# A trunk of convolution, attention and gated layers: layer norm read from PSUM, two output jobs side by side, one PSUM layout

## The chip, the core and the metric

The kernel runs on one core of a Trainium2 chip. A core has a matrix engine (PE, whose weight loads stand apart as PEld), a vector engine (DVE), a scalar engine (ACT), a general engine (POOL) and a queue engine that starts transfers (SP). Each works through its own queue of instructions in order and waits for the others by semaphores. SBUF is the working memory; PSUM is the small memory that the matrix engine writes its sums to, eight banks of 512 numbers of 4 bytes in each of 128 partitions. POOL cannot read or write PSUM in this kernel's program: all its operands lie in SBUF.

The metric is the time of one execution on the device, in microseconds (us). Lower is better.

## What is computed

The input is 256 positions of 2048 features. There is one convolution layer with its gated feed-forward block, then keys and values, then one attention layer with its feed-forward block, and a last norm. The change lies in the convolution layer alone:

```python
def _conformer_conv(h, w1, b1, dw, dw_b, ln_g, ln_b, w2, b2):
    u = h @ w1 + b1
    a, gate = jnp.split(u, 2, axis=-1)
    u = a * jax.nn.sigmoid(gate)
    u = lax.conv_general_dilated(...) + dw_b
    u = jax.nn.silu(_layernorm(u, ln_g, ln_b))
    return u @ w2 + b2

def _layernorm(x, g, b):
    mu = jnp.mean(xf, axis=-1, keepdims=True)
    var = jnp.mean(jnp.square(xf - mu), axis=-1, keepdims=True)
    y = (xf - mu) * lax.rsqrt(var + LN_EPS) * g + b
```

The convolution runs over the positions, feature by feature, with 31 taps. Its layer norm needs every feature of a position, so that no number of z = silu(layernorm(...)) exists before the last tile of features has been through product, gate and convolution.

## The kernel before

Features lie on the partitions, in 16 tiles of 128; the 256 positions are the columns. All matrix products are of 4-byte numbers split in a high part (`hi`, cast by ACT on L168) and a rest (`lo`, made on L170 by DVE or POOL): three passes, hi by hi, hi by rest and rest by hi. The weights come in blocks of 512 KB, 4 tiles of inputs by 256 outputs, started by SP through a ring of four `raw` buffers, with three `whi` and three `wlo` buffers behind it. `next_block` hands out a block and prepares those up to two further on (`AHEAD`), in the order of the list `blocks`.

**First product (w1).** 16 jobs, j = 0 to 15, each of four blocks (L480, `project`, matmuls on L223). The first block of a job is native: its four tiles take one pass of unsplit weights (`rawn`). Job j makes 128 features and their 128 gates in one PSUM bank, `pp` of shape 128 x 2 x 256, and three such banks go round. Then `glu(bk, j)`, called with high priority: DVE scales the bank by the norm (L380), ACT makes the gate (L382), DVE multiplies and writes `up[:, j]` (L383). While the next job runs on PE, `conv(j)` works on `up[:, j]`: ACT starts two sums in PSUM (L409, `acc`, two tiles called `aux`), DVE adds 23 taps to them in turn (L411), ACT and POOL make six taps by products and a tree of sums (L423, L425, L442, L444), and DVE puts them together into `cT[:, j]` (L447). The last job differs: 16 taps go through PE with diagonal weights (L404) and 12 through ACT and DVE. `set_shift` (L455) sums `cT[:, 0]` on PE to get a shift that later tiles subtract, and `stats(j)` sums `cT[:, j]` and its squares over the features on PE (L474, L476, L478) into the tile `st`.

**Layer norm and z.** Behind the last statistics an order written out by hand holds for ACT, DVE and POOL: ACT copies the mean from PSUM to `mu` in SBUF (L509), DVE squares it and subtracts (L511, L512), ACT takes the root (L513), DVE and POOL subtract `mu` (L517; POOL takes the tiles 2 to 15 in seven pairs), DVE takes the reciprocal (L518). Then group after group (two single tiles, seven pairs): DVE scales (L522), ACT takes Silu (L530), ACT or DVE casts the high part of z (L531), DVE makes the rest (L532).

**Second product (w2).** Eight jobs u of four blocks (L341, matmuls on L227 and L229), each making 256 features in two banks, two such tiles going round; `residual` reads them (L331, L333). The stages behind it (feed-forward, attention, feed-forward) use the same `project`.

PSUM has two layouts, one after the other: three `pp` of one bank with five `aux`, then, from L534 on, two `pp` of two banks with four `aux`.

What the program as built waits for is a matter of the framework: it follows which instruction touches which part of a tile and puts a semaphore wait where two engines touch the same one. It also chooses the order of each engine's queue outside the part that is ordered by hand.

Of the kernel before, what the change touches and what calls it, by code (L numbers as in the profile page):

```python
# [12 lines left out]
ALU = mybir.AluOpType  # L13
# [66 lines left out]
def trunk(ctx: ExitStack, tc: tile.TileContext, xT, vec, const, w1, w2, wk, wv, wq, wo, wg0, wu0, wd0, wg1, wu1, wd1, out):  # L80
# [46 lines left out]
    for u in range(DT // 2):  # L127
        plan(w2, u, DT)
# [17 lines left out]
    def emit_block():  # L146
        i = len(ready)
        w, u, g, gk = blocks[i]
        shape = [P, gk, GK * NB // gk]
        native = NATIVE if w is w1 and g == 0 else 0  # L150
        if native:
            raw = conv_pool[0].tile(shape, F32, name="rawn", bufs=2)
        else:
            raw = wp.tile(shape, F32, name="raw", bufs=RAW)
        hi = lo = None
        if native < gk:
            hi = wp.tile(shape, F32R, name="whi", bufs=AHEAD + 1)
            lo = wp.tile(shape, F32R, name="wlo", bufs=AHEAD + 1)
        src = w[u, g].rearrange("p (k n) -> p k n", k=gk)
        step = gk if i >= DT // GK else 1 if i == 0 else 2  # L160
        for s in range(0, gk, step):
            if i < DT // GK:
                load_x(GK * g + s, step)
            part = slice(s, s + step)
            nc.sync.dma_start(raw[:, part, :], src[:, part, :])
            part = slice(max(s, native), s + step)
            if part.start < part.stop:
                nc.scalar.copy(hi[:, part, :], raw[:, part, :])  # L168
                eng = nc.gpsimd if (w is w1 and i >= 6) or (w is w2 and u == 0) else nc.vector
                eng.tensor_tensor(out=lo[:, part, :], in0=raw[:, part, :], in1=hi[:, part, :].bitcast(F32), op=ALU.subtract)  # L170
        ready.append((raw, hi, lo))
        if i == DT // GK - 1:
            x_loaded()

    def next_block(w, u, g):
        i = used[0]
        used[0] += 1
        assert blocks[i][:3] == (w, u, g)
        while len(ready) < min(len(blocks), i + 1 + AHEAD):
            emit_block()  # L180
        return ready[i]
# [18 lines left out]
    psum = []  # L200

    def bank2():
        return psum[-1].tile([P, 2, 2, S], F32, name="pp", bufs=2)

    def aux(shape):
        return psum[-1].tile(shape, F32, name="aux", bufs=4 if len(psum) > 1 else 5)

    def project(w, u, kt_n, x, xf=None):


        bk = psum[-1].tile([P, 2, S], F32, name="pp", bufs=3) if xf is not None else bank2()
# [20 lines left out]
        return bk  # L232

# [102 lines left out]
    def out_proj(w, kt_n, x, bias, g):  # L336

        nx = new_x(rp, "x")
        norm = Norm()
        for u in range(DT // 2):  # L340
            residual(project(w, u, kt_n, x), u, bias, norm)  # L341
            for i in (2 * u, 2 * u + 1):
                split_scaled(nx, i, v(g, i))
        return nx, norm
# [6 lines left out]
    with tc.tile_pool(name="cv", bufs=1) as cv, tc.tile_pool(name="cvu", bufs=1) as cvu:  # L351
        conv_psum = ExitStack()
        psum.append(conv_psum.enter_context(tc.tile_pool(name="psc", bufs=1, space=PSUM)))
# [37 lines left out]
        def conv(j):  # L391
# [3 lines left out]
            acc = [aux([P, S]) for _ in range(3 if n_pe else 2)]  # L395
# [17 lines left out]
            def products(lo, hi):  # L413
                for k in range(lo, hi):
# [5 lines left out]
                    else:  # L420
                        win, w = tap(TAPS - n_pool + k)
                        if k == 0:
                            nc.scalar.activation(dst, win, AF.Identity, scale=w, bias=v("dw_b", j))  # L423
                        else:
                            nc.scalar.activation(dst, win, AF.Copy, scale=w)  # L425

            def step(n):
# [3 lines left out]
                if n == 0 and n_pe:  # L431
                    on_pe()
                if n < 2:
                    products(*((0, 4) if n == 0 else (4, leaves)))
                for i in range(n_vec):
                    if i * 4 // n_vec == n:
# [21 lines left out]

        st = aux([P, 2, S])
# [20 lines left out]
        for j in range(DT):  # L480
            bk = project(w1, j, DT, x, xf)
# [13 lines left out]
            if j == DT - 1:  # L495
                table(AF.Sqrt, sigmoid)
# [4 lines left out]
        flush()  # L501

# [4 lines left out]
        with tc.manual_schedule(engines={mybir.EngineType.Activation, mybir.EngineType.DVE, mybir.EngineType.Pool}):  # L507
            mu = cv.tile([P, S], F32, name="mu")
            nc.scalar.copy(mu, st[:, 0, :])  # L509
            rl = sp.tile([P, S], F32, name="rstd")  # L510
            nc.vector.tensor_tensor(out=rl, in0=mu, in1=mu, op=ALU.mult)  # L511
            nc.vector.tensor_tensor(out=rl, in0=st[:, 1, :], in1=rl, op=ALU.subtract)  # L512
            nc.scalar.activation(rl, rl, AF.Sqrt, bias=ln_eps)  # L513
            groups = [(0, 1), (1, 1)] + [(j, 2) for j in range(2, DT, 2)]
            for j, n in groups:
                c2 = cT[:, j:j + n, :]
                (nc.vector if j < 2 else nc.gpsimd).tensor_tensor(out=c2, in0=c2, in1=_bc(mu, n), op=ALU.subtract)  # L517
            nc.vector.reciprocal(rl, rl)  # L518

            def scaled(j, n):  # L520
                c2 = cT[:, j:j + n, :]
                nc.vector.tensor_tensor(out=c2, in0=c2, in1=_bc(rl, n), op=ALU.mult)  # L522

            scaled(*groups[0])
            for i, (j, n) in enumerate(groups):
# [6 lines left out]
                nc.vector.tensor_tensor(out=z[:, j:j + n, 1, :], in0=c2, in1=z[:, j:j + n, 0, :].bitcast(F32), op=ALU.subtract)  # L532

        conv_psum.close()  # L534
        psum.append(ctx.enter_context(tc.tile_pool(name="ps", bufs=1, space=PSUM)))
        x, norm = out_proj(w2, DT, z, "b2", "f0_g")
# [178 lines left out]
```

## Time and profile before

| | us |
|---|---|
| median of 3 runs | 2209.11 (2209.0 to 2209.14) |
| the profiled execution | 2208.4 |
| its span in the trace | 2206.6 |
| PE busy | 2173.5 (98%) |
| DVE busy | 1297.3 (59%) |
| ACT busy | 1071.0 (49%) |
| POOL busy | 463.4 (21%) |

In a row of the timeline the first number is the start and the second the length in us; several equal instructions that follow each other are one row, with their count behind an x, and the square brackets tell how long the engine had been idle and who released it. The chain of waits goes back from the last instruction of the program, at each step to what it had waited for. An fp32 matmul of unsplit numbers stands twice in the records (x16 for 8).

### The profile page before, as it was taken

Reading aid. Unit: us, or ns where it says so; the run is one execution under the profiler, and the core shown is the slowest. Engines: PE = TensorE matmul, PEld = TensorE weight load, DVE = VectorE, ACT = ScalarE, POOL = GpSimd, SP = SyncE. Lnnn points to the kernel's source line nnn. Section 1 sums busy time; section 2 is a strip of 40 time slices with the busy share of each in tenths; the row PEclk is TensorE's granted clock in tenths of the full one; section 3 lists DMA queues with packets and bytes.
Section 4 is the critical chain, followed back from the end, with each engine's and each line's share of the span. In section 5 each row is a group of like instructions: output and inputs, shape, how many; then the busy total and the mean of one; then the engine's idle time right before and its main releaser. Section 6 shows DMA issues by size and latency. Waiting matters only on the chain.

```text
span 2206.6 us, 31780 instructions
## 1 busy us (share of the span) xinstructions
PE 2173.5 (98%) x12570; PEld 1916.9 (87%) x12570; DVE 1297.3 (59%) x1626; ACT 1071.0 (49%) x1393; POOL 463.4 (21%) x296
## 2 busy tenths in 40 slices
PE   8999799999999999999999999999999999999997
PEld 7999688888888888888888888888888888888886
DVE  7888876555555554555545677665555555544444
ACT  6666455444444444444444566454444444443442
POOL 5999211212121210000000100112121212100000
PEclk9999899999999999999999999999999999999999
DMA  6544355555555555555565544555555555555553
GB/s 235 172 167 158 106 187 185 190 185 189 190 188 189 187 191 190 186 188 190 181 192 192 188 143 136 189 190 186 188 190 189 186 188 190 189 187 188 191 190 125
DMA packets 112181, 401.41 MB, mean 182 GB/s; under 512 B 12576, under 2 KB 13728, under 8 KB 112032
## 3 DMA queue, kind: packets, MB, share of 16 engines
q1 hardware_dynamic: 111456, 398.57, 54.7%
q8 instruction: 98, 1.61, 0.3%
q10 hardware_dynamic: 576, 0.81, 0.1%
q14 instruction: 51, 0.42, 0.1%
HBM read 397.24 MB, written 2.10 MB: 181 GB/s over the span
## 4 chain that ended last, share of the span: by engine, by line
PE 97%; DVE 1%; issue 0%; ACT 0%; DMA 0%; SPq 0%; DVEq 0%; ACTq 0%
PE pp L227 54%; PE pp L229 28%; PE pp L223 8%; PE pp L262 1%; PE pp L264 1%; PE pp L263 1%; PE pp L245 1%; PE pp L247 0%; PE aux L598 0%; PE aux L593 0%; PE aux L575 0%; PE aux L474 0%; DVE x L278 0%; DMA hT<-xT 0%; DVE x L663 0%
## 5 line engine op out<-in xcount | busy, mean ns | idle before, releaser
L170 DVE TENSOR_TENSOR wlo<-raw,whi 128x1024 fp32r<-128x1024 f32 (+1 forms) x691 | 860.8, 1246 | 797.3 <-ACT whi L168 796.8
L168 ACT CAST whi<-raw 128x1024 fp32r<-128x1024 f32 (+1 forms) x739 | 772.7, 1046 | 1034.9 <-PE pp L227 816.7
L227 PE MATMUL pp<-x,whi 128*128 128x512 f32 x3328 | 839.4, 393 | 0.0
L227 PEld LDWEIGHTS pp<-x,whi 128*128 128x128 f32 x3328 | 599.4, 189 | 106.6
L229 PEld LDWEIGHTS pp<-x,wlo 128*128 128x128 f32 x3328 | 454.0, 190 | 32.4
L229 PE MATMUL pp<-x,wlo 128*128 128x256 f32 x3328 | 464.1, 282 | 0.0
L227 PE MATMUL pp<-hid,whi 128*128 128x512 f32 x1320 | 330.5, 392 | 0.0
L227 PEld LDWEIGHTS pp<-hid,whi 128*128 128x128 f32 x1320 | 237.4, 189 | 42.4
L300 POOL TENSOR_TENSOR sqacc<-sqacc,sq 128x512 f32<-128x512 f32 x30 | 50.6, 1688 | 711.5 <-ACT sq L296 701.6
L229 PEld LDWEIGHTS pp<-hid,wlo 128*128 128x128 f32 x1320 | 180.1, 190 | 12.9
L229 PE MATMUL pp<-hid,wlo 128*128 128x256 f32 x1320 | 184.1, 282 | 0.0
L553 POOL TENSOR_TENSOR hid<-t,hid 128x512 fp32r<-128x512 f32 x44 | 79.7, 1810 | 396.1 <-ACT hid L552 396.1
L411 DVE SCALAR_TENSOR_TENSOR aux<-up,vecs,aux 128x256 f32<-128x256 f32 x355 | 144.5, 480 | 3.4 <-ACT aux L409 3.4
L223 PE MATMUL pp<-x,whi 128*128 128x256 f32 x768 | 142.1, 287 | 1.1 <-ACT whi L168 1.1
L547 POOL TENSOR_TENSOR t<-t,rstd 128x512 f32<-128x512 f32 x44 | 57.0, 1297 | 352.8 <-DVE t L272 343.9
L223 PEld LDWEIGHTS pp<-x,whi 128*128 128x128 f32 x768 | 120.7, 191 | 2.4 <-ACT whi L168 1.5
L170 POOL TENSOR_TENSOR wlo<-raw,whi 128x1024 fp32r<-128x1024 f32 x48 | 114.0, 2390 | 24.4 <-DVE up L383 14.9
L223 PE MATMUL pp<-x,wlo 128*128 128x256 f32 x384 | 109.2, 284 | 4.9 <-DVE wlo L170 4.9
L223 PEld LDWEIGHTS pp<-x,wlo 128*128 128x128 f32 x384 | 73.5, 191 | 6.3 <-DVE wlo L170 5.9
L227 PE MATMUL pp<-z,whi 128*128 128x512 f32 x256 | 67.7, 406 | 10.8 <-DVE z L532 10.7
L272 DVE TENSOR_TENSOR t<-pp,t 128x512 f32<-128x512 f32 x104 | 71.0, 683 | 6.1 <-ACT t L271 6.1
L549 POOL TENSOR_TENSOR t<-t,rstd 128x512 f32<-128x512 f32 x44 | 65.3, 1484 | 34.3 <-ACT t L548 34.3
(130 smaller groups left out, 1505.7 us busy)
## 6 DMA issues: line engine op xcount, KB each, us to landing
raw<-wg SPq DMA_DIRECT2D x176, 512.0 KB, 3.3
raw<-wu SPq DMA_DIRECT2D x176, 512.0 KB, 3.3
raw<-wd SPq DMA_DIRECT2D x176, 512.0 KB, 3.3
raw<-w SPq DMA_DIRECT2D x77, 512.0 KB, 3.3
raw<-wv SPq DMA_DIRECT2D x32, 512.0 KB, 4.1
raw<-wk SPq DMA_DIRECT2D x32, 512.0 KB, 3.4
raw<-wq SPq DMA_DIRECT2D x32, 512.0 KB, 3.3
raw<-wo SPq DMA_DIRECT2D x32, 512.0 KB, 3.3
```

Source lines behind the costliest of these rows:

```text
L168: nc.scalar.copy(hi[:, part, :], raw[:, part, :])
L170: eng.tensor_tensor(out=lo[:, part, :], in0=raw[:, part, :], in1=hi[:, part, :].bitcast(F32), op=ALU.subtract)
L223: nc.tensor.matmul(bk[:, m, :], a[:, j, ws], b, start=first and m == 0 and i == 0, stop=last and i == len(passes) - 1, skip_group_check=True)
L227: nc.tensor.matmul(bk[:, m, :, :], hi[:, j, ws], x[:, kt, :, :], start=kt == 0, stop=False, skip_group_check=True)
L229: nc.tensor.matmul(bk[:, m, 0, :], lo[:, j, ws], x[:, kt, 0, :], start=False, stop=kt == kt_n - 1, skip_group_check=True)
L245: nc.tensor.matmul(bk[:, 0, :, :], hi[:, j, :], x[:, kt, :, :], start=kt == 0, stop=False, skip_group_check=True)
L272: nc.vector.tensor_tensor(out=t, in0=bk[:, :, 0, :], in1=t, op=ALU.add)
L300: add.tensor_tensor(out=self.acc, in0=self.acc, in1=sq, op=ALU.add)
L411: nc.vector.scalar_tensor_tensor(out=acc[i % 2], in0=win, scalar=w, in1=acc[i % 2], op0=ALU.mult, op1=ALU.add)
L547: nc.gpsimd.tensor_tensor(out=t, in0=t, in1=_bc(norm.r, 2), op=ALU.mult)
L549: nc.gpsimd.tensor_tensor(out=t, in0=t, in1=_bc(norm.r, 2), op=ALU.mult)
L553: nc.gpsimd.tensor_tensor(out=hid[:, 2 * u:2 * u + 2, 1, :], in0=o, in1=hid[:, 2 * u:2 * u + 2, 0, :].bitcast(F32), op=ALU.subtract)
```

## The change

- `psum` is one pool for the whole program: two `pp` of two banks and four `aux`. The convolution stage takes both `pp`: `jobs`, whose two halves (a bank each) serve the jobs j of w1 in turn, and `chains`, whose two banks hold the two tap sums of the odd j. The even j keep two `aux`.
- The first two jobs of w2 run side by side: their blocks alternate in the list, and `project_pair` is a generator that issues two tiles of inputs for both jobs at a time and is stepped once for each group of z behind the first. The blocks from the fourth of these eight on are prepared at five places in the loop over the groups; one more than before is prepared ahead of the statistics. Their `lo` parts are all made by POOL.
- The layer norm reads the mean (`st[:, 0, :]`) and the reciprocal deviation (`st[:, 1, :]`, where DVE now writes it) from PSUM in DVE's own steps. ACT squares the mean from PSUM; `mu` in SBUF stays for POOL's seven pairs.
- In the last convolution ACT starts the sums ahead of the products, and the load of the root's table moves from behind the last gate to behind the last product.
- `out_proj` takes the two finished jobs as `first`.

Nothing of the arithmetic is left out, and the number of matmuls and of transfers stays.

```diff
...
         plan(w1, u, DT)
-    for u in range(DT // 2):
+    for g in range(DT // GK):
+        blocks.extend((w2, u, g, GK) for u in range(2))
+    for u in range(2, DT // 2):
...
                 nc.scalar.copy(hi[:, part, :], raw[:, part, :])
-                eng = nc.gpsimd if (w is w1 and i >= 6) or (w is w2 and u == 0) else nc.vector
+                eng = nc.gpsimd if (w is w1 and i >= 6) or (w is w2 and u < 2) else nc.vector
...
-    def next_block(w, u, g):
+    def next_block(w, u, g, ahead=AHEAD):
...
         assert blocks[i][:3] == (w, u, g)
-        while len(ready) < min(len(blocks), i + 1 + AHEAD):
+        while len(ready) < min(len(blocks), i + 1 + ahead):
...
-    psum = []
+    psum = ctx.enter_context(tc.tile_pool(name="ps", bufs=1, space=PSUM))
     def bank2():
-        return psum[-1].tile([P, 2, 2, S], F32, name="pp", bufs=2)
+        return psum.tile([P, 2, 2, S], F32, name="pp", bufs=2)
     def aux(shape):
-        return psum[-1].tile(shape, F32, name="aux", bufs=4 if len(psum) > 1 else 5)
...
-    def project(w, u, kt_n, x, xf=None):
...
-        bk = psum[-1].tile([P, 2, S], F32, name="pp", bufs=3) if xf is not None else bank2()
+        return psum.tile(shape, F32, name="aux", bufs=4)
...
+    def project(w, u, kt_n, x, xf=None, bk=None):
...
+        if bk is None:
+            bk = bank2()
...
+    def project_pair(w, x, bks):
...
+        for g in range(DT // GK):
+            parts = [next_block(w, u, g, 0)[1:] for u in range(2)]
+            for s in range(0, GK, 2):
+                tiles = [(g * GK + j, j, m, slice(m * P, (m + 1) * P)) for j in range(s, s + 2) for m in range(2)]
+                for bk, (hi, lo) in zip(bks, parts):
+                    for kt, j, m, ws in tiles:
+                        nc.tensor.matmul(bk[:, m, :, :], hi[:, j, ws], x[:, kt, :, :], start=kt == 0, stop=False, skip_group_check=True)
+                for bk, (hi, lo) in zip(bks, parts):
+                    for kt, j, m, ws in tiles:
+                        nc.tensor.matmul(bk[:, m, 0, :], lo[:, j, ws], x[:, kt, 0, :], start=False, stop=kt == DT - 1,
+                                         skip_group_check=True)
+                yield
...
-    def out_proj(w, kt_n, x, bias, g):
+    def out_proj(w, kt_n, x, bias, g, first=()):
...
         for u in range(DT // 2):
-            residual(project(w, u, kt_n, x), u, bias, norm)
+            residual(first[u] if u < len(first) else project(w, u, kt_n, x), u, bias, norm)
...
     with tc.tile_pool(name="cv", bufs=1) as cv, tc.tile_pool(name="cvu", bufs=1) as cvu:
-        conv_psum = ExitStack()
-        psum.append(conv_psum.enter_context(tc.tile_pool(name="psc", bufs=1, space=PSUM)))
+        jobs, chains = bank2(), bank2()
...
             n_vec = TAPS - n_pool - n_pe
-            acc = [aux([P, S]) for _ in range(3 if n_pe else 2)]
+            acc = [chains[:, i, 0, :] if j % 2 else aux([P, S]) for i in range(2)] + [aux([P, S])] * (n_pe > 0)
...
                         if k == 0:
-                            nc.scalar.activation(dst, win, AF.Identity, scale=w, bias=v("dw_b", j))
+                            i = nc.scalar.activation(dst, win, AF.Identity, scale=w, bias=v("dw_b", j))
                         else:
-                            nc.scalar.activation(dst, win, AF.Copy, scale=w)
+                            i = nc.scalar.activation(dst, win, AF.Copy, scale=w)
+                        last_product[:] = [i.ins]
...
                     on_pe()
+                vector = [i for i in range(n_vec) if i * 4 // n_vec == n]
+                if n_pe:
+                    for i in vector:
+                        on_vector(n_pe + i, i)
...
                     products(*((0, 4) if n == 0 else (4, leaves)))
-                for i in range(n_vec):
-                    if i * 4 // n_vec == n:
+                if not n_pe:
+                    for i in vector:
...
+        last_product = []
...
         for j in range(DT):
-            bk = project(w1, j, DT, x, xf)
+            bk = project(w1, j, DT, x, xf, jobs[:, j % 2, :, :])
...
                         set_diag(k)
-            if j == DT - 1:
-                table(AF.Sqrt, sigmoid)
...
         flush()
+        emit_block()
+        table(AF.Sqrt, last_product[-1])
...
         with tc.manual_schedule(engines={mybir.EngineType.Activation, mybir.EngineType.DVE, mybir.EngineType.Pool}):
+            bks = [bank2(), bank2()]
+            pair = project_pair(w2, z, bks)
             mu = cv.tile([P, S], F32, name="mu")
+            rl = sp.tile([P, S], F32, name="rstd")
+            groups = [(0, 1), (1, 1)] + [(j, 2) for j in range(2, DT, 2)]
...
+            def centred(j, n, eng, m):
+                c2 = cT[:, j:j + n, :]
+                eng.tensor_tensor(out=c2, in0=c2, in1=_bc(m, n), op=ALU.subtract)
...
+            def scaled(j, n):
+                c2 = cT[:, j:j + n, :]
+                nc.vector.tensor_tensor(out=c2, in0=c2, in1=_bc(st[:, 1, :], n), op=ALU.mult)
...
+            nc.scalar.activation(rl, st[:, 0, :], AF.Square)
             nc.scalar.copy(mu, st[:, 0, :])
-            rl = sp.tile([P, S], F32, name="rstd")
-            nc.vector.tensor_tensor(out=rl, in0=mu, in1=mu, op=ALU.mult)
+            centred(*groups[0], nc.vector, st[:, 0, :])
...
             nc.scalar.activation(rl, rl, AF.Sqrt, bias=ln_eps)
-            groups = [(0, 1), (1, 1)] + [(j, 2) for j in range(2, DT, 2)]
-            for j, n in groups:
-                c2 = cT[:, j:j + n, :]
-                (nc.vector if j < 2 else nc.gpsimd).tensor_tensor(out=c2, in0=c2, in1=_bc(mu, n), op=ALU.subtract)
-            nc.vector.reciprocal(rl, rl)
...
-            def scaled(j, n):
-                c2 = cT[:, j:j + n, :]
-                nc.vector.tensor_tensor(out=c2, in0=c2, in1=_bc(rl, n), op=ALU.mult)
+            centred(*groups[1], nc.vector, st[:, 0, :])
+            for j, n in groups[2:]:
+                centred(j, n, nc.gpsimd, mu)
+            nc.vector.reciprocal(st[:, 1, :], rl)
...
-        conv_psum.close()
-        psum.append(ctx.enter_context(tc.tile_pool(name="ps", bufs=1, space=PSUM)))
-        x, norm = out_proj(w2, DT, z, "b2", "f0_g")
+                if j in (4, 6, 8, 10, 12):
+                    emit_block()
+                if j:
+                    next(pair)
...
+        x, norm = out_proj(w2, DT, z, "b2", "f0_g", bks)
...
```

Where the instructions stand, before and now (each row is a line, an operation, what it writes and reads; waits in square brackets; an x and a number for equal rows that follow each other).

PE's queue between the w1 jobs 3 and 4, before, with the semaphores that each row waits for (`rawn` is the native block, `cst` the constants):

```order
L223 MATMUL pp<-x,wlo 128x256
L223 MATMUL pp<-xf,rawn 128x256 [waits DMAHW4_49]
L223 MATMUL pp<-xf,rawn 128x256 x7
L474 MATMUL aux<-cT,cst 128x256 [waits Pool_49]
L223 MATMUL pp<-x,whi 128x256 [waits Activation_49]
```

The same place now:

```order
L226 MATMUL pp<-x,wlo 128x256
L497 MATMUL aux<-cT,cst 128x256 [waits Pool_49]
L497 MATMUL aux<-cT,cst 128x256 [waits DVE_49]
L226 MATMUL pp<-xf,rawn 128x256 [waits DMAHW4_49,DVE_49]
L226 MATMUL pp<-xf,rawn 128x256 x7
```

The first matmul of the job has a wait for DVE that it did not have, and the statistics have moved from behind the native block to ahead of it. Counting DVE's signals in the two programs tells which instruction the wait is for: now it is the last step of the gated unit of the job just before, L400 of job j - 1, at every j from 1 to 15; before it was L383 of job j - 3, from job 5 on.

DVE's queue from the end of the statistics to the third group of z, before (`rstd` is the working tile of the deviation, `aux` the PSUM tile of the statistics):

```order
L511 TENSOR_TENSOR rstd<-mu 128x256
L512 TENSOR_TENSOR rstd<-aux,rstd 128x256
L517 TENSOR_TENSOR cT<-cT,mu 128x256 x2
L518 RECIPROCAL rstd<-rstd 128x256
L522 TENSOR_TENSOR cT<-cT,rstd 128x256 x2
L532 TENSOR_TENSOR z<-cT,z 128x256
L522 TENSOR_TENSOR cT<-cT,rstd 128x512
```

And now:

```order
L539 TENSOR_TENSOR cT<-cT,aux 128x256
L549 TENSOR_TENSOR rstd<-aux,rstd 128x256
L539 TENSOR_TENSOR cT<-cT,aux 128x256
L554 RECIPROCAL aux<-rstd 128x256
L543 TENSOR_TENSOR cT<-cT,aux 128x256 x2
L564 TENSOR_TENSOR z<-cT,z 128x256
L543 TENSOR_TENSOR cT<-cT,aux 128x512
```

One step (the square) has left DVE, and the subtractions and scalings have one operand in PSUM where both were in SBUF.

ACT's queue over the later groups of z, before (L530 is Silu, L168 the cast of a weight block):

```order
L530 ACTIVATE cT<-cT,vecs 128x256 x6
L168 CAST whi<-raw 128x1024
L530 ACTIVATE cT<-cT,vecs 128x256 x4
L168 CAST whi<-raw 128x1024
L530 ACTIVATE cT<-cT,vecs 128x256 x4
```

And now:

```order
L562 ACTIVATE cT<-cT,vecs 128x256 x4
L170 CAST whi<-raw 128x1024
L562 ACTIVATE cT<-cT,vecs 128x256 x2
L170 CAST whi<-raw 128x1024
L562 ACTIVATE cT<-cT,vecs 128x256 x2
L170 CAST whi<-raw 128x1024
```

Five casts of w2 blocks now stand between the Silus, one for each pair of tiles, and POOL has their five `lo` parts in a row behind its seven subtractions, where it had one.

## The prediction

> **What bounds the kernel now.** The page's chain of waits comes first.
>
> ```profile
> PE 97%; DVE 1%; issue 0%; ACT 0%; DMA 0%; SPq 0%; DVEq 0%; ACTq 0%
> ```
>
> PE ends the kernel, so an edit pays where PE stands still and costs where PE is made to. The chain in order of time shows the w1 jobs (8 native matmuls in 16 records, 72 others, 88 in all, with the statistics of an earlier tile between):
>
> ```profile
> 25.01 1.05 PE aux L307 x4
> 30.32 18.12 PE pp L223 x134
> 48.44 0.43 PE aux L455 x2
> 192.84 12.08 PE pp L223 x88
> 204.93 0.43 PE aux L474 x2
> 205.36 8.52 PE pp L223 x71
> ```
>
> A job is 12.08 + 0.43 = 12.51 us without a gap, and w1 ends at 205.36 + 8.52 = 213.9. The timeline then has the only long pause of PE:
>
> ```profile
> 215.94 7.18 PE L404 MATMUL aux<-up,diag 128*128 128x256 f32 x32 [0.23 <-DVE up L383]
> 223.80 0.42 DVE L447 TENSOR_TENSOR cT<-aux,cT 128x256 f32<-128x256 f32 x1
> 224.81 0.61 PE L478 MATMUL aux<-sq,cst 128*128 128x256 f32 x2
> 225.91 9.76 POOL L517 TENSOR_TENSOR cT<-cT,mu 128x512 f32<-128x512 f32 x7 [5.59 <-ACT mu L509]
> 226.74 2.36 DVE L517 TENSOR_TENSOR cT<-cT,mu 128x256 f32<-128x256 f32 x2
> 229.02 1.74 DVE L518 RECIPROCAL rstd<-rstd 128x256 f32<-128x256 f32 x1
> 234.68 1.19 PE L227 MATMUL pp<-z,whi 128*128 128x512 f32 x2 [9.26 <-DVE z L532]
> 263.02 2.00 PE L227 MATMUL pp<-z,whi 128*128 128x512 f32 x8
> ```
>
> The statistics end at 225.4, the first matmul of w2 comes at 234.68, and job 2 of w2 starts at 263.02. From the end of w1 to there it is 49.1 us. In steady state a w2 block takes the step between 260.23 and 263.02, 2.79 us:
>
> ```profile
> 260.23 2.00 PE L227 MATMUL pp<-z,whi 128*128 128x512 f32 x8
> ```
>
> Two jobs are eight such blocks, 22.3 us, so some 27 of the 49 are the change's target.
>
> **Part 1: a new wait in all w1 jobs but the first.** Before, PE started job j while DVE and ACT worked on the gated unit of job j - 1, three banks going round. Now, by the program's waits (shown with the change), PE may begin job j only when L400 of job j - 1 has written `up`, though the two jobs use different banks of `jobs`: the halves of one tile are treated as one. How long that takes after a job's last matmul, the boundary at 201.3 shows:
>
> ```profile
> 201.31 3.62 PE L223 MATMUL pp<-xf,rawn 128*128 128x256 f32 x16
> 201.51 0.70 DVE L380 TENSOR_TENSOR pp<-pp,rstd 128x512 f32<-128x512 f32 x1 [1.39 <-PE pp L223]
> 202.38 0.47 ACT L382 ACTIVATE gate<-pp,vecs 128x256 f32<-128x256 f32 x1
> 202.90 0.48 DVE L383 SCALAR_TENSOR_TENSOR up<-pp,vecs,gate 128x256 f32<-128x256 f32 x1
> ```
>
> PE went on at 201.31; the unit ends at 202.90 + 0.48 = 203.38. With the 0.05 us from L383's end (215.41 + 0.48) to L404's start at 215.94, PE loses 2.12 us. The statistics of 0.43 us now stand ahead of the wait and lie inside it. A job takes 12.08 + 2.12 = 14.20 in place of 12.51: **1.69 us more**. Behind the waiting matmul stand all 88 of the job; ACT's casts wait for the buffers that they free, and nothing there runs short, having 1.69 us more per job.
>
> Does DVE reach L397 in time? Its longest stretch is 20 tap steps of 144.5 / 355 = 0.407 us:
>
> ```profile
> L411 DVE SCALAR_TENSOR_TENSOR aux<-up,vecs,aux 128x256 f32<-128x256 f32 x355 | 144.5, 480 | 3.4 <-ACT aux L409 3.4
> ```
>
> They start some 5.2 us after the job's end (2.1 for the unit, four tap steps, two L469, a start by ACT) and last 8.1: 13.3, less than 14.20. So DVE stands ready.
>
> The first two boundaries differ. Job 1 started at 25.88, paused for weights until 30.32, and ended at about 30.32 + 72 x 0.118 = 38.8.
>
> ```profile
> 25.88 3.62 PE L223 MATMUL pp<-xf,rawn 128*128 128x256 f32 x16
> 30.18 0.48 DVE L383 SCALAR_TENSOR_TENSOR up<-pp,vecs,gate 128x256 f32<-128x256 f32 x1
> 32.90 4.80 DVE L411 SCALAR_TENSOR_TENSOR aux<-up,vecs,aux 128x256 f32<-128x256 f32 x12 [2.23 <-ACT aux L409]
> ```
>
> Now it starts at 30.18 + 0.48 + 0.05 = 30.7, the weights being there by then, and ends at 42.8. Next PE meets the shift's matmul (L477), moved up to this place, which waits for `cT[:, 0]`: 23 tap steps of 4.80 / 12 = 0.40 from 32.90 and two L469 end at 42.9. DVE's order puts L397 of job 1 behind these, and the unit takes 1.87 (201.51 to 203.38): 44.8. So job 2 ends at 44.85 + 12.08 = 56.9, and 13 jobs of 14.20 later w1 ends at 241.5, against 213.9: **+27.6**.
>
> **Part 2: from the end of w1 to job 2 of w2.** The table load moves off ACT's path to the last tile, but the third sum of that tile waits for PE's diagonal matmuls (215.94 + 7.18 = 223.1), as its start depends on L400 as before. So the last L469 ends at 223.6 in place of 224.2, and the statistics at 224.8: 10.9 after the end of w1, 0.6 earlier.
>
> From there the steps, at the durations of their likes:
>
> ```profile
> 225.46 0.37 ACT L509 COPY mu<-aux 128x256 f32<-128x256 f32 x1 [0.79 <-PE aux L478]
> 226.40 0.42 DVE L512 TENSOR_TENSOR rstd<-aux,rstd 128x256 f32<-128x256 f32 x1
> 226.86 0.51 ACT L513 ACTIVATE rstd<-rstd,vecs 128x256 f32<-128x256 f32 x1 [1.02 <-DVE rstd L512]
> 231.76 0.60 ACT L530 ACTIVATE cT<-cT,vecs 128x256 f32<-128x256 f32 x1 [3.09 <-DVE cT L522]
> 232.39 0.41 ACT L531 CAST z<-cT 128x256 fp32r<-128x256 f32 x1
> ```
>
> ACT's square and copy 0.8; DVE's L539 (it waits for the copy: both read one PSUM tile) and L549 0.85; the root 0.5; the reciprocal 1.7; a scaling 0.4; Silu and cast 1.0; with the gaps 5.6. The rest of z takes 0.4, or up to 1.4 where it waits for POOL: 6.5 in place of 9.3. DVE steps with one operand in PSUM don't wait for POOL, and a cast in SBUF does:
>
> ```profile
> 218.25 2.08 POOL L444 TENSOR_TENSOR prod<-prod 128x512 f32<-128x512 f32 x2
> 219.30 3.61 DVE L411 SCALAR_TENSOR_TENSOR aux<-up,vecs,aux 128x256 f32<-128x256 f32 x9
> 242.50 2.39 POOL L170 TENSOR_TENSOR wlo<-raw,whi 128x1024 fp32r<-128x1024 f32 x1 [6.83 <-ACT whi L168]
> 242.82 2.36 DVE L531 CAST z<-cT 128x512 fp32r<-128x512 f32 x1 [0.36 <-ACT cT L530]
> ```
>
> The tap steps beside POOL kept 0.40 each; L531 lasted until POOL's 2.39 were over. The Trainium skill, "SBUF — State Buffer", section "Who interferes with whom", has it as a rule: a DVE instruction with two SBUF inputs, or in a two-port mode, and a GpSimd one that reads SBUF shut each other out for a whole instruction. By that rule, with which the rows agree, the PSUM operands free only the subtractions and scalings, and the five `lo` parts on POOL hold up the casts and rests of z: it speaks against this part of the change.
>
> Then the pair: 22.3 of matmuls, about 1 for the second tile of z, and three losses. POOL's `lo` parts come two at a time, as PE frees buffers, so that the cast and the rest of a pair of z each wait for one: with 2.39 a part, PE then waits some 2.4 for z, at two of the eight steps. Second, both jobs end together and both PSUM tiles are full: job 2 of w2 waits for three L349 and one L351, less the 0.5 by which the first job ends earlier:
>
> ```profile
> 254.60 0.88 DVE L331 SCALAR_TENSOR_TENSOR hT<-pp,vecs,hT 128x256 f32<-128x256 f32 x2 [2.29 <-PE pp L229]
> 256.53 0.68 DVE L333 TENSOR_TENSOR hT<-pp,hT 128x512 f32<-128x512 f32 x1
> ```
>
> That is 1.3 + 0.7 - 0.5 = 1.5. Third, the granted clock (the last number but two):
>
> ```profile
> 12.00:16.00 4.00, 1.70 (x12) 1.50 (x12) 4.00 (x4) 3.59 (x9) 3.71 (x3) 1.00 1.05 399
> 231.00:233.00 2.00, 0.00 (x0) 0.00 (x0) 2.00 (x2) 1.00 (x2) 2.00 (x3) 0.50 0.00 0
> 243.00:245.00 2.00, 2.00 (x9) 1.61 (x8) 2.00 (x1) 0.77 (x2) 1.89 (x1) 0.78 0.00 0
> ```
>
> It falls to half in the pause and is back only within 243 to 245. The pause gets shorter by 3 but stays over 6, so the first matmuls of the pair still run at half speed: about 3 us. The sum is 10.9 + 6.5 + 22.3 + 1 + 4.8 + 1.5 + 3 = 50.0, against 49.1. **+0.9 at this end**; if z never waits for POOL and the clock stays, 42.2, which is **-6.9**; if z waits for POOL a third time and the clock is back a little later, 53, **+4**. I take 50, since L531's row shows the full block.
>
> **The rest.** The stages behind w2 have the same instructions in the same order on all engines, at the same count of transfers, and PSUM there is as before; nothing is costed. SP's order moves one native block by four places in w1, where PE now has 1.69 us more per job. POOL's three `lo` parts of a job (2.4 each) now always follow its product tree, as in the last jobs before, where PE had no gap (the piece at 192.84).
>
> **The sum.** 2208.4 + 27.6 + 0.9 = 2236.9, made against the profiled execution (span 2206.6, 1.8 around it); the median of the runs shown is 0.7 higher. A measurement of this kernel can tell about 0.2%, 4.4 us, from no change. I put the time at 2236.
>
> **Rivals.** *The wait is not felt (faster).* If the signal that PE waits for stood for the unit of two jobs ago, it would be up before each job starts, w1 would stay at 213.9, and the other end decides: 2208.4 + 0.9 down to 2208.4 - 6.9, with its middle at 2205. The point is where the unit's end falls: anything later than 0.43 us (the statistics) behind the last matmul is lost time. For it speaks only that job and unit use different banks; against it, that the program's count names the job just before at all 15 boundaries. 0.05 for faster by more than 0.2%, 0.02 within.
>
> *The clock falls in w1 too.* If each pause of 2.1 us halved the clock for some 3 us of matmuls, each of 14 jobs would lose 1.5 more: 2236 + 21 = 2257. The Trainium skill, "TensorE: Matmul & The Clock Gate", section "What's actually happening", puts the fall at an idle window of about 3.4 us, and its section "A second HAM failure mode: psum-queue depth-cycling" tells of a kernel whose short pauses made the clock swing. Against it stands the stretch 12 to 16 above: PE busy for 1.70 of 4 us at a granted clock of 1.00. 0.05.
>
> *The pair pays in full.* Part 2's best end: 2208.4 + 27.6 - 6.9 = 2229. L531's row speaks against it. 0.15.
>
> *The boundary costs more.* Should weight loads and the start of matmuls after each wait cost another 0.2 and the second part its upper end, the sum is 2208.4 + 30.2 + 4 = 2242.6. 0.1.
>
> **How the numbers follow.** The forecast, 2231 to 2240, has 0.63. With the full pair and the dearer boundary the range is 2227 to 2243, leaving out the unfelt wait and the clock, 0.12 together, and a little of either edge. Slower by over 0.2% holds all but the first rival: 0.93; within 0.2% 0.02; faster 0.05.
>
> **What would show it.** In w1 the chain of waits should show the gated unit (L397, L399, L400) between pieces of 12.1 us on PE, at a period of 14.2; PE's idle time ahead of L226 should name `up`, DVE L400, 14 or 15 times. L477 should start near 43, w1 end near 241.5. PE's first matmul on z should come 17.4 us after the end of w1, job 2 of w2 49 to 51 us after it, behind a wait for L351; DVE's L563 and L564 should reach lengths over 2 us beside POOL's L172. A period of 12.5 in w1 would make part 1 wrong; a clock below 1.00 between 45 and 240 would bring in the second rival.

## The result, and the profile after

| | before | after |
|---|---|---|
| median, us | 2209.06 (4 runs) | 2243.18 (4 runs, 2242.34 to 2246.03) |
| profiled execution, us | 2208.4 | 2246.03 |
| span of it, us | 2206.6 | 2244.0 |

The change makes the kernel slower: ratio 1.0158 (95% interval 1.0145 to 1.017), +34.1 us in the medians. The forecast was 2236, with 2227 to 2243 around it: the direction came out, and 2243.18 lies 7.2 above the one and just above the other. The profiled execution is the longest of its four, 2.9 above their median, so its sums come out that much higher.

The page's chain of waits by engine is of little help here. It can be followed back only to 283.5 us, in the second stage, and shows nothing of what lies ahead:

```profile
PE 86%; DVE 1%; DVEq 0%; ACT 0%; issue 0%
```

What PE waited for between 20 and 330 us says more (total us, times, longest):

```profile
PE pp L226 <- DVE up L400: 26.9, 15, 4.7
PE pp L245 <- DVE z L564: 10.8, 4, 6.0
PE pp L230 <- DVE hT L351: 1.6, 1, 1.6
```

The first row is new: 15 waits for the gated unit, one for each w1 job but the first. The timeline of PE shows the starts of jobs 1, 2, 3, 4 and 15, and the statistics that follow the last matmul of w1:

```profile
31.28 6.18 PE L226 MATMUL pp<-xf,rawn 128*128 128x256 f32 x16 [4.67 <-DVE up L400]
48.04 3.72 PE L226 MATMUL pp<-xf,rawn 128*128 128x256 f32 x16 [1.52 <-DVE up L400]
62.48 5.41 PE L226 MATMUL pp<-xf,rawn 128*128 128x256 f32 x16 [2.09 <-DVE up L400]
78.47 3.72 PE L226 MATMUL pp<-xf,rawn 128*128 128x256 f32 x16 [1.09 <-DVE up L400]
236.69 3.72 PE L226 MATMUL pp<-xf,rawn 128*128 128x256 f32 x16 [1.66 <-DVE up L400]
248.88 0.60 PE L497 MATMUL aux<-cT,cst 128*128 128x256 f32 x2
```

w1 ends at 248.88, against 213.9 before: **+35.0**, where I had +27.6. The 16 native matmul records that took 3.62 us before take 3.72 after a pause, and at jobs 1 and 3 they take 6.18 and 5.41: PE's clock is halved there. One boundary, on DVE and ACT:

```profile
234.64 0.70 DVE L397 TENSOR_TENSOR pp<-pp,rstd 128x512 f32<-128x512 f32 x1 [0.53 <-PE pp L226]
235.25 1.01 DVE L428 SCALAR_TENSOR_TENSOR pp<-up,vecs,pp 128x256 f32<-128x256 f32 x2
235.51 0.47 ACT L399 ACTIVATE gate<-pp,vecs 128x256 f32<-128x256 f32 x1
236.16 0.48 DVE L400 SCALAR_TENSOR_TENSOR up<-pp,vecs,gate 128x256 f32<-128x256 f32 x1
```

The gate is there at 235.98, but DVE is in two taps into `chains` and reaches L400 at 236.16. At every other boundary the two taps go to `aux` and take 0.87; PE's starts are then 14.31 us apart, here 14.44.

The second stage, on PE (the four waits), POOL and DVE:

```profile
266.35 1.22 PE L245 MATMUL pp<-z,whi 128*128 128x512 f32 x2 [6.03 <-DVE z L564]
280.15 2.14 PE L245 MATMUL pp<-z,whi 128*128 128x512 f32 x8 [2.30 <-DVE z L564]
288.39 3.40 PE L245 MATMUL pp<-z,whi 128*128 128x512 f32 x8 [2.30 <-DVE z L564]
300.31 2.06 PE L230 MATMUL pp<-z,whi 128*128 128x512 f32 x8 [1.57 <-DVE hT L351]
274.64 4.91 POOL L172 TENSOR_TENSOR wlo<-raw,whi 128x1024 fp32r<-128x1024 f32 x2 [4.37 <-PE pp L248]
275.28 2.05 DVE L563 CAST z<-cT 128x512 fp32r<-128x512 f32 x1 [2.21 <-ACT cT L562]
277.37 2.72 DVE L564 TENSOR_TENSOR z<-cT,z 128x512 fp32r<-128x512 f32 x1
```

The first matmul on z comes 17.5 us after w1 (20.8 before), the pair from there to job 2 takes 34.0 (28.3 before): 51.4 in all, against 49.1.

### The profile page after: what moved, and what is told of

It is laid out like the page before. It is cut to its first block, busy times and chain, and to the rows that moved or that the text cites. A ratio compares the mean times of both kernels' runs of the same rounds, so it can differ in the third digit from the quotient of the medians.

```text
span 2244.0 us, 31783 instructions
## 1 busy us (share of the span) xinstructions
PE 2184.1 (97%) x12570; PEld 1922.0 (86%) x12570; DVE 1313.1 (59%) x1621; ACT 1070.7 (48%) x1394; POOL 473.0 (21%) x300
## 4 chain that ended last, share of the span: by engine, by line
PE 86%; DVE 1%; DVEq 0%; ACT 0%; issue 0%
PE pp L230 52%; PE pp L232 27%; PE pp L281 1%; PE pp L280 1%; PE pp L282 1%; PE pp L263 1%; PE pp L265 0%; PE pp L245 0%; PE aux L632 0%; PE aux L627 0%; PE aux L609 0%; DVE x L697 0%; PE aux L608 0%; PE aux L633 0%; PE aux L325 0%; PE pp L248 0%
## 5 line engine op out<-in xcount | busy, mean ns | idle before, releaser
L172 POOL TENSOR_TENSOR wlo<-raw,whi 128x1024 fp32r<-128x1024 f32 x52 | 123.8, 2390 | 38.2 <-DVE up L400 14.9
L581 POOL TENSOR_TENSOR t<-t,rstd 128x512 f32<-128x512 f32 x44 | 57.0, 1296 | 352.4 <-DVE t L290 352.4
L428 DVE SCALAR_TENSOR_TENSOR pp<-up,vecs,pp 128x256 f32<-128x256 f32 x171 | 83.6, 489 | 22.2 <-ACT pp L426 16.9
L226 PE MATMUL pp<-xf,rawn 128*128 128x256 f32 x256 | 66.2, 417 | 30.7 <-DVE up L400 26.9
L226 PEld LDWEIGHTS pp<-xf,rawn 128*128 128x128 f32 x256 | 52.0, 208 | 44.3 <-DVE up L400 32.8
L428 DVE SCALAR_TENSOR_TENSOR aux<-up,vecs,aux 128x256 f32<-128x256 f32 x184 | 74.0, 482 | 2.2 <-ACT aux L426 2.2
```

What stands on the lines that cost most here:

```text
L226: nc.tensor.matmul(bk[:, m, :], a[:, j, ws], b, start=first and m == 0 and i == 0, stop=last and i == len(passes) - 1, skip_group_check=True)
L428: nc.vector.scalar_tensor_tensor(out=acc[i % 2], in0=win, scalar=w, in1=acc[i % 2], op0=ALU.mult, op1=ALU.add)
L581: nc.gpsimd.tensor_tensor(out=t, in0=t, in1=_bc(norm.r, 2), op=ALU.mult)
```

## Experiments

Each ran on one chip with the kernel before beside it: 2208.96 for the first four, 2208.91 for the next four, 2208.61 for the last two.

**1. The halves as tiles of their own.** The changed kernel with separate PSUM tiles; the two-bank tiles of w2 come from a pool opened behind the convolution.

```diff
...
-        jobs, chains = bank2(), bank2()
+        jobs = [psc.tile([P, 2, S], F32, name=f"job{i}") for i in range(2)]
+        chains = [psc.tile([P, 2, S], F32, name=f"chain{i}") for i in range(2)]
...
-            bk = project(w1, j, DT, x, xf, jobs[:, j % 2, :, :])
+            bk = project(w1, j, DT, x, xf, jobs[j % 2])
...
```

> The changed kernel, with the two halves of `jobs` and of `chains` as tiles of their own, a bank each. If PE's wait for the gated unit of the job just before is all that part 1 costs, the jobs of w1 follow each other without a gap again (a start every 12.5 us against 14.4), no half clock shows between 30 and 210 us, w1 ends at 213.9 +/- 0.7 as before the change, and the time is that of before plus what the second stage has lost in the trace of the changed kernel (51.4 against 49.1 us): 2209 + 2.3 = 2211. Rival: the layout itself (four banks for the accumulators in place of five, two for the chains) holds w1 up as well; then w1 ends at 217 or later, and the time is 2215 or more.

Measured: 2208.89, ratio 1.0004 (0.9995 to 1.0013). The start of a late job on PE:

```profile
189.02 3.62 PE L227 MATMUL job<-xf,rawn 128*128 128x256 f32 x16
```

The period is 12.51 us again, no half clock shows in w1, and w1 ends at 214.0. All of the loss of w1 is gone; the second stage takes 48.5 us here (one long wait in the pair in place of two), so that in the medians the rest of the change nets nothing. The eleven executions lie in two groups, six at 2208.1 to 2208.9 and five at 2210.5 to 2211.8. The trace is of one of the six; what the five lose, perhaps the second long wait that the changed kernel has, is not shown.

**2. The halves alone, in the kernel before.**

```diff
...
+        jobs = psum[-1].tile([P, 2, 2, S], F32, name="pp", bufs=1)
...
-            bk = project(w1, j, DT, x, xf)
+            bk = project(w1, j, DT, x, xf, jobs[:, j % 2, :, :])
```

> The kernel before, with one edit: the w1 jobs go to the two halves of one two-bank tile in turn. If this wait alone is part 1, w1 shows a period of 14.3 to 14.5 us, a job 1 of which the first matmuls run at half clock, and ends 33 to 35 us later than before, at 247 to 249; the stage behind it stays at 49 us, and the time is 2242 to 2244. Rival: the wait costs what I had worked out (2.12 a boundary, no clock): +27.6, 2236.6; the rest then belongs to other parts of the change.

Measured: 2243.25, ratio 1.0156 (1.0142 to 1.017), the time of the whole change. The first two pauses, on PE:

```profile
32.01 5.41 PE L224 MATMUL pp<-xf,rawn 128*128 128x256 f32 x16 [4.67 <-DVE up L385]
48.01 5.41 PE L224 MATMUL pp<-xf,rawn 128*128 128x256 f32 x16 [1.96 <-DVE up L385]
```

Here jobs 1 and 2 run at half clock, where it was 1 and 3 in the changed kernel; the later period is 14.35. With the first run, this shows that part 1 is the whole loss. Nor is it the number of banks: run 1 has two in turn for the jobs as well, where the kernel before has three, and keeps the period of 12.51.

**3. The layer norm from PSUM alone, in the kernel before** (L509 to L522 as in the changed kernel, the two PSUM layouts kept).

> The kernel before, with the mean and reciprocal deviation of the layer norm read from PSUM and nothing else of the change. If that part does what it says, the first matmul on z comes 17.5 us after the end of w1 in place of 20.8, the two jobs of w2 behind it still take 28.3, and the time is 2209 - 3.3 = 2205.7. Rival: the gain is eaten at the next step, because the later tiles of z are no sooner there (POOL still takes the mean from 14 of them, one after the other): job 2 of w2 then starts 49 us after the end of w1 as before, and the time is 2209.

Measured: 2214.53, ratio 1.0025 (1.0015 to 1.0034): slower, which neither theory had. PE's wait:

```profile
PE pp L227 <- DVE cT L518: 17.8, 1, 17.8
```

The releaser is not z but the last scaling. The reciprocal now lies in a bank of the old layout, all scalings read it there, and w2's tiles of the second layout lie over that bank: the first matmul waits until the last tile is scaled. So this part needs a PSUM layout that stays, as the change has it (run 6 shows the rest).

**4. The `lo` parts of the pair on DVE** (the kernel of run 1, `(w is w2 and u < 2)` dropped from the choice of POOL).

> As the first of these runs, with the `lo` parts of the first two jobs of w2 made by DVE in place of POOL. If PE's two waits of 2.3 us for z come from casts and rests of z that stand still while POOL makes a `lo` part, both waits go, and with the second of them the half clock behind it (1.6): the stage behind w1 takes 51.4 - 4.6 - 1.6 = 45.2 us, and the time is 2211 - 6.2 = 2205. Rival: the waits come from weight buffers that PE frees late, and the casts of z would be late with DVE as busy as that anyway: the stage stays above 50, and the time at 2210 or more.

Measured: 2208.41, ratio 0.9996 (0.9987 to 1.0005). PE's waits for z are down to the first one and 0.3, but a new one stands ahead of the statistics; the second fence is DVE's timeline there:

```profile
PE aux L501 <- DVE cT L473: 2.7, 1, 2.7
```

```profile
224.56 0.41 DVE L473 TENSOR_TENSOR cT<-chain,prod 128x256 f32<-128x256 f32 x1
224.90 1.21 DVE L172 TENSOR_TENSOR wlo<-raw,whi 128x1024 fp32r<-128x1024 f32 x1
226.03 0.41 DVE L473 TENSOR_TENSOR cT<-chain,cT 128x256 f32<-128x256 f32 x1
```

Three of the eight parts fall among the last taps and sums: the first matmul on z comes 3.7 us later (234.92 against 231.20), the pair takes 27.9 in place of 31.3, and one cancels the other.

**5. Matmuls in PE's pauses.** The changed kernel, with matmuls into a spare bank that nothing reads; `chains` shares one bank for that.

```diff
...
+            if j:
+                fill(9 if j == 1 else 4)
             bk = project(w1, j, DT, x, xf, jobs[:, j % 2, :, :])
```

> The changed kernel, with matmuls that nothing reads put into PE's pauses in w1: nine ahead of job 1, four ahead of each later one (0.45 us each); for their bank the two chains share one. The wait for the gated unit stays. If the half clock at job 1 and at one later job comes from PE's standing still, no half clock shows between 30 and 210 us, the first matmuls of job 1 take 3.6 us in place of 6.2, those of the other jobs 3.6 in place of 3.7, and w1 ends at about 243.5 in place of 248.9; the time is 2238 to 2240. Rival: the slow matmuls are slow for another reason (weights or transfers of that moment); then they stay, and the time is 2243 or, with the matmuls added, a little more.

Measured: 2247.85, ratio 1.0176 (1.0163 to 1.019). PE at the first pauses:

```profile
26.65 6.64 PE L379 MATMUL spare<-xf,cst 128*128 128x256 f32 x30
33.17 3.72 PE L227 MATMUL jobs<-xf,rawn 128*128 128x256 f32 x16
45.36 2.32 PE L379 MATMUL spare<-xf,cst 128*128 128x256 f32 x10
47.95 3.62 PE L227 MATMUL jobs<-xf,rawn 128*128 128x256 f32 x16
```

The clock stayed at full speed to the end of w1, as expected, and job 1's matmuls take 3.72 in place of 6.18. The time came out worse, since the framework put later jobs' matmuls forward: 15 (in 30 records) at job 1 and four to six at each of the next nine, which outlast the wait; w1 ends at 250.3 against 248.9 in the changed kernel. The mechanism is shown, its price is not; run 9 repeats it with fewer.

**6. The kernel of run 1 without the pair.**

> The first run's kernel (a tile for each half) without the pair: the jobs of w2 one after the other as before, the layer norm from PSUM, and the accumulators' banks of the layer norm not handed over to w2. If the loss of the run with the layer norm alone came from PE's waiting for the banks of the old layout (the last scaling that reads PSUM), it is gone here: the first matmul on z comes 17.1 us after the end of w1, the two jobs take 28.3, and the time is 2209 - 3.7 = 2205.3. Rival: reading the mean and the reciprocal from PSUM makes the later tiles of z late by itself; then PE waits at the second or third tile for more than 3 us, and the time stays at 2209 or above.

Measured: 2205.93, ratio 0.9986 (0.9978 to 0.9995). PE's first matmuls on z, w1 having ended at 215.20:

```profile
232.35 2.54 PE L229 MATMUL pp<-z,whi 128*128 128x512 f32 x4 [6.12 <-DVE z L565]
236.76 2.08 PE L229 MATMUL pp<-z,whi 128*128 128x512 f32 x4 [1.88 <-DVE z L565]
```

17.15 us after w1, and job 2 of w2 at 261.06, 28.7 later. What is left of the change here is worth 3.0 us, and the pair, as it stands in run 1, loses just that in the medians (2208.89). Not all of the 3.0 is the layer norm's: the reordered last convolution is in this run too, and the statistics end 11.0 us after w1 in place of 11.6. From their end to the first matmul on z it is 6.1 in place of 9.3, and this is the part of the reading from PSUM.

**7. Five of the eight `lo` parts on DVE**, in the kernel of run 1.

```diff
...
-                eng = nc.gpsimd if (w is w1 and i >= 6) or (w is w2 and u < 2) else nc.vector
+                eng = nc.gpsimd if (w is w1 and i >= 6) or (w is w2 and 2 * g + u < 3) else nc.vector
...
```

> The first run's kernel, with only those five of the eight `lo` parts of the pair made by DVE that are due once the layer norm has begun; the first three stay on POOL. If the run with all eight on DVE lost at the statistics (three parts among the last taps, 3.7 us) what it gained at z, this one keeps the gain alone: first matmul on z 17.1 us after w1, job 2 of w2 27.9 after that (31.3 with POOL), and the time is 2208.9 - 3.4 = 2205.5. Rival: the gain at z came from z being later as a whole, with the weights long there; then the two jobs take 30 or more again, and the time is 2208 to 2209.

Measured: 2204.36, ratio 0.9979 (0.997 to 0.9987). PE's first step and job 2 of w2:

```profile
231.20 4.25 PE L246 MATMUL pp<-z,whi 128*128 128x512 f32 x8 [6.13 <-DVE z L570]
257.82 2.06 PE L231 MATMUL pp<-z,whi 128*128 128x512 f32 x8 [1.57 <-DVE hT L352]
```

26.6 from z to job 2, against 31.3: with no `lo` part on POOL beside them, the casts and rests of z hold nobody up. It was POOL, and in the medians the pair now gains 1.6 over run 6.

**8. Run 7, with matmuls that nothing reads in the pause ahead of z, and the pair's last step in the order of the jobs.**

> As the run with five `lo` parts on DVE, with twelve matmuls that nothing reads in PE's pause ahead of z, and with the last step of the pair in the order of the jobs, so that job 0's bank is full 1.4 us before job 1's. If the half clock at the first step comes from the pause, that step takes 2.8 us in place of 5.2 to 5.7; if the wait for L351 comes from both jobs' ending together, it shrinks from 1.6 to about 0.2. Both: 2205.5 - 2.7 - 1.4 = 2201.4. Rival: the pause's matmuls hold up the statistics or the first step, and the bank wait is ended by the other job's residual anyway: 2205.

Measured: 2202.96, ratio 0.9973 (0.9962 to 0.9984), the lowest median of all. PE, and behind it DVE ahead of job 2:

```profile
226.23 5.34 PE L541 MATMUL aux<-sq,cst 128*128 128x256 f32 x24
232.53 1.16 PE L248 MATMUL pp<-z,whi 128*128 128x512 f32 x4 [0.95 <-DVE z L577]
237.00 2.12 PE L248 MATMUL pp<-z,whi 128*128 128x512 f32 x8 [0.99 <-DVE z L577]
258.35 2.08 PE L231 MATMUL pp<-z,whi 128*128 128x512 f32 x8 [1.39 <-DVE hT L355]
```

```profile
255.59 0.87 DVE L353 SCALAR_TENSOR_TENSOR hT<-pp,vecs,hT 128x256 f32<-128x256 f32 x2 [2.38 <-PE pp L252]
256.39 1.21 DVE L172 TENSOR_TENSOR wlo<-raw,whi 128x1024 fp32r<-128x1024 f32 x1
257.52 0.68 DVE L355 TENSOR_TENSOR hT<-pp,hT 128x512 f32<-128x512 f32 x1
```

The first step takes 3.5 us in place of 5.2, at full clock, but PE then runs into z and waits 0.99. The bank wait hardly shrinks, a miss: DVE has a `lo` part between L353 and L355.

**9. Run 5 with fewer matmuls in the pauses of w1**, on the native weights of the job that follows.

```diff
...
+                for _ in range(8 if u == 1 else 3):
+                    nc.tensor.matmul(spare, raw[:, 0, 0:P], xf[:, 0, :], start=True, stop=True)
...
```

> As the run with matmuls in the pauses, but fewer, so that they end before the wait does: eight ahead of job 1, three or four ahead of most later jobs (six ahead of job 2), on the native weights of the job that follows. The wait itself stays. If the half clock is what the first boundary was short by in my sum, job 1's first matmuls take 3.6 to 3.7 us in place of 6.2, job 2 starts at about 46.2 in place of 48.0, no half clock shows between 30 and 240, w1 ends near 243.6 in place of 248.9, and the time is 2239 to 2240 against 2243.2. Rival: what the clock gives back is lost to the matmuls in the pauses, and the time is 2243 or above, as in the run with more of them.

Measured: 2241.65, ratio 1.0148 (1.0133 to 1.0164). Jobs 1 and 2 on PE:

```profile
31.50 3.72 PE L230 MATMUL jobs<-xf,rawn 128*128 128x256 f32 x16 [1.22 <-DVE up L409]
46.28 3.62 PE L230 MATMUL jobs<-xf,rawn 128*128 128x256 f32 x16
```

Job 2 starts at 46.28 (46.2 expected), no half clock shows in w1, and w1 ends at 245.9, 3.0 before the changed kernel's (243.6 was expected, and 2239 to 2240 for the time). In the medians 1.5 is left of it, and the two intervals overlap: that the clock costs is shown in the traces, its share of the median is not settled.

**10. The kernel of run 1 with only `jobs` in two tiles**, `chains` still one.

> As the first run, but with `chains` still one tile of two banks and only `jobs` in two. If the wait of w1 hangs on `jobs` alone, w1 has its period of 12.5 us and the time is that of the first run, 2209, though the taps into `chains` go on taking 0.52 us each in place of 0.40. Rival: the tie of the two chains (each first tap waits for both starts by ACT, and taps are slower) makes DVE late for the unit; then the period is 12.8 or more and the time 2214 or above.

Measured: 2216.77, ratio 1.0037 (1.0024 to 1.0049). The rival's time, but not its place: the period is 12.51, and most of the loss stands behind w1 (23.9 us to the first matmul on z, 17.2 in run 1), on DVE and as a wait of PE:

```profile
220.19 4.00 DVE L432 SCALAR_TENSOR_TENSOR aux<-up,vecs,aux 128x256 f32<-128x256 f32 x10
225.55 4.15 DVE L432 SCALAR_TENSOR_TENSOR chains<-up,vecs,chains 128x256 f32<-128x256 f32 x8
```

```profile
PE aux L501 <- DVE cT L473: 4.2, 1, 4.2
```

Ten taps into `aux` take 4.00, eight into `chains` 4.15: that fits a tap into one half that waits for the tap just before, into the other. Between taps into `aux`, those into `chains` start 0.39 apart from their neighbours (DVE's rows from 207.68 to 214.34), and in run 1, with a tile for each chain, eight of them take 3.22. The last chain also starts late, at 224.10 against 217.59. So the change has a second tie, worth 7.9 us, and the first one hides most of it: with 1.9 us more per job, DVE has time for the slower taps.

## Why the prediction was right in kind and short in size

- **The mechanism held.** PE waits for L400 of the job before at 15 boundaries, the rest of the change nets to nothing, and w1 decides. Runs 1 and 2 show it from both sides.
- **The term that failed is the +27.6 of w1; it measured +35.0.** Three steps of it were short. First, "a job takes 12.08 + 2.12 = 14.20": it takes 14.31 and 14.44 in turn, as the first matmuls after a pause need 0.1 more and two taps into `chains` hold L400 up by 0.13 at every other boundary; over 13 jobs +2.3. Second, the start: "job 2 so starts at 44.85", and it started at 48.04. Job 1 began 0.6 late, since DVE made a `lo` part ahead of L400 (the two rows below), and its first matmuls then took 2.6 us more at half clock, which I had priced at z but not here, though the pause was in my own sum. Third, a half clock at job 3, +1.7. With 0.1 in the last job: 2.3 + 3.2 + 1.7 + 0.1 = 7.3 of the 7.4.

```profile
29.62 1.22 DVE L172 TENSOR_TENSOR wlo<-raw,whi 128x1024 fp32r<-128x1024 f32 x1
30.75 0.48 DVE L400 SCALAR_TENSOR_TENSOR up<-pp,vecs,gate 128x256 f32<-128x256 f32 x1
```

- **The second stage held, in part by luck.** 17.4 to the first matmul on z was 17.5, but the statistics came 11.4 us after w1 where I had 10.9, as ten taps of the last chain take 5.21 in `chains`, and the way from there took 6.0 where I had 6.5. Two waits of 2.4 were 2.30 each, the bank wait of 1.5 was 1.57, L563 and L564 stretched to 2.05 and 2.72. The clock fell twice, not once: 51.4 for 50.0. In the medians (run 1 against before) the part is worth -0.1 where I had +0.9, with the two groups of run 1 on either side of that.
- **What I gave nothing for, `chains`,** cost little only because part 1's pauses cover it (run 10: 7.9 us without them).
- **The clock rival** was too coarse both ways. I had it at every pause or at none, and held a row of 4 us with PE 1.70 busy against it. That row was just on the harmless side, as the last section shows.

That 2243.18 is under the profiled 2246.03 fits fewer falls of the clock in the other executions: their mean granted clock is 0.993 to 0.994, against 0.992 in the profiled one. They have no traces, so this stays argued.

## What to carry to other kernels

Before two halves of one tile go to two engines in turn, look at the program's waits: the framework may tie them, and a tie between PE and a chain of DVE and ACT costs the whole chain at each turn. When a change puts a short pause into a dense stretch, price the clock by how busy the pause leaves its stretch, not by its length alone. When one loss is found, undo its parts one by one: a second may lie in its shadow, and a gain (here -3.0, in run 6) may need another edit to show.

## What the runs showed of the clock

The half clock falls at instants 3.413 us apart, and what counts is PE's busy time in the stretch just before. Stretches of the changed kernel (length, then PE's busy time; the clock is the last number but two):

```profile
26.06:29.47 3.41, 0.55 (x3) 0.14 (x1) 2.21 (x2) 2.69 (x3) 0.00 (x0) 1.00 0.23 90
60.19:63.60 3.41, 1.32 (x7) 1.02 (x6) 3.07 (x7) 2.56 (x5) 2.92 (x2) 1.00 0.59 209
63.60:67.02 3.42, 3.42 (x10) 2.68 (x9) 3.28 (x9) 2.56 (x7) 1.52 (x3) 0.50 0.50 167
90.91:94.32 3.41, 1.75 (x9) 1.25 (x8) 3.29 (x7) 3.01 (x7) 3.00 (x2) 1.00 0.78 275
285.47:288.88 3.41, 1.11 (x7) 0.86 (x7) 3.38 (x4) 0.00 (x0) 2.32 (x1) 1.00 0.59 163
```

Of the kernel before (its clock falls at 230.25, which gives the instants), of run 2 and of run 4:

```profile
11.79:15.20 3.41, 1.67 (x12) 1.50 (x12) 3.41 (x4) 3.41 (x8) 3.33 (x3) 1.00 1.05 395
223.42:226.83 3.41, 1.71 (x7) 0.76 (x5) 1.56 (x5) 0.79 (x2) 0.92 (x1) 1.00 0.00 0
```

```profile
45.99:49.41 3.42, 1.46 (x8) 1.25 (x8) 1.18 (x2) 2.84 (x6) 2.93 (x2) 1.00 0.62 207
```

```profile
8.93:12.33 3.40, 1.54 (x7) 0.87 (x5) 2.39 (x3) 2.45 (x6) 2.88 (x3) 1.00 0.99 358
```

The clock fell at 29.47, 63.60 and 288.88, which are 10 and 66 such stretches apart. It fell behind stretches with PE busy for 0.55, 1.32, 1.11, 1.46 (run 2) and 1.54 us (run 4) of 3.41, and not behind 1.67, 1.71 or 1.75: in these traces the limit lies between 45% and 49%. In the twelve traces, no stretch at full clock from 10 us on breaks this. A pause of 2.1 us that falls wholly into one stretch, with no statistics beside it, leaves 1.32. With statistics the stretch keeps 1.75, and where an instant cuts the pause in two (run 2, 1.97 us, cut at 63.06) the stretches keep 2.81 and 2.04: neither does harm. This is why one boundary of the 14 behind job 1 was hit, and another one in run 2. The Trainium skill, "TensorE: Matmul & The Clock Gate", section "What's actually happening", has the free-running window of 3413 ns, which these rows confirm; it lets the clock fall after an idle window, and here a window 45% busy was enough.
